# Latent attention: the causal corner masked by eight extra rows of the score product, query and key pages in fixed tiles

## The chip, the cores and the metric

The kernel runs on one core of a Trainium2 chip. The metric is the device time of one execution in microseconds (us). The core's engines run side by side, each with its own queue of instructions: PE multiplies matrices (its weight loads are listed as PEld), DVE does vector work, ACT evaluates functions, POOL does further vector work, and SP issues most of the DMA transfers. PE writes its products to PSUM; everything else lies in SBUF, which has 128 partitions.

## The reference

One encoder layer on a sequence of 1024 rows of 1024 values. The mixer has eight latent heads and eight chunk-band heads; a gated MLP with a short convolution follows. Only the latent heads' attention is touched:

```python
def mla_attention(q, k, v):                      # q, k: 8 heads of 96 values (64 + 32 rotary)
    scale = Dq ** -0.5
    key_chunk = jnp.arange(S) // CHUNK           # CHUNK = 64
    def block(args):                             # one block of 128 queries
        qi, i = args
        s = jnp.einsum('bqhd,bkhd->bhqk', qi, k) * scale
        q_chunk = (i * Q_BLOCK + jnp.arange(Q_BLOCK)) // CHUNK
        mask = key_chunk[None, :] <= q_chunk[:, None]
        s = jnp.where(mask[None, None], s, NEG_INF)
        p = jax.nn.softmax(s, axis=-1)
        return jnp.einsum('bhqk,bkhd->bqhd', p, v)
```

A query block of 128 rows holds two chunks of 64. Keys up to the end of the block are used, and the first 64 queries must not see the last 64 of these keys: a corner of 64 x 64 in each block's score tile.

## The kernel before

**Stages.** The program first computes the modulation and the projections, then the chunk-band heads, then the latent heads, then the output projection and the MLP. In the profile the latent score products (L807) start between 367 us and 583 us; their values products (L895) follow until about 599 us.

**Numbers.** A 32-bit operand is split into a high and a low half, and a product is made of three: high x high, high x low, low x high. All three accumulate in one PSUM tile.

**Pages.** A page is 512 rows of queries or of keys, transposed, so that the head's values lie on the partitions. `qk_page` (L736) builds one for the latent heads: four transposes on PE into PSUM (`page_psum`, L733), the high half by ACT (L741 for queries, L745 for keys), the low half by DVE (L742, L746). A latent page uses 96 partitions. `ca_pages` (L749) does the same for a pair of chunk-band heads and uses all 128. Query pages come from a tag with four buffers (`q2`), key pages from a tag with three buffers, each buffer with high and low half; the buffers are taken in turn.

**Units and tiles.** A `Unit` is one head and one group `g` of four query blocks. There are 16 chunk-band units, then 16 latent ones in the order group 0, group 1 of each head. Each has four score tiles, so that there are 64 latent score tiles. For a latent tile `scores` (L778) issues the products (L807), sets the masked corner of the PSUM tile to 1e30 (DVE, L825), takes the row minimum (DVE, L826; scores are negated, so that the minimum plays the part of the maximum), the exponential and its row sum (ACT, L833), the reciprocal and its scaling (DVE, L835 and L836), then the high half of the probabilities (POOL, in the helper at L73) and the low half (DVE, L855), and their transpose by DMA (L867). `values`, three tiles later, multiplies the transposed probabilities with the values (PE, L895), and ACT and DVE (L904, L905) bring the sum out. The score tiles alternate between two PSUM buffers.

**Order.** The units' tiles are written out in a loop; between them `pace` adds steps of the low-priority projections (`fillers`: among them `f_up` with L666 to L694, `f_oca` with L154 to L156). Pages of the next unit are prepared at the third tile of a unit if the projection that they need has been written out by then, otherwise right before the unit's first tile; the first latent head's two pages of each kind are in the latter case. The order of instructions on each engine is then set by a planner that goes by priorities (`tc.high_priority`), by dependencies and by a model of each instruction's time, so that other work of an engine may stand between two instructions that follow each other in the text.

Of the kernel before, what the change touches and what calls it, by code (L numbers as in the profile page):

```python
# [14 lines left out]
F32R = mybir.dt.float32r  # L15
# [7 lines left out]
MUL, ADD, SUB, MIN, MAX = ALU.mult, ALU.add, ALU.subtract, ALU.min, ALU.max  # L23

P = 128
D = 1024
S = 1024
NT = S // P
# [2 lines left out]
NF = FF // P  # L31
EPS = 1e-6
BIG = 1e30
QR, KVR, ROPE, NOPE, VD = 256, 128, 32, 64, 64
QK = NOPE + ROPE
HD = 64
# [28 lines left out]
def layer_kernel(ctx, tc, I, out):  # L65
    nc = tc.nc
    pe, act, dve, pool, sp = nc.tensor, nc.scalar, nc.vector, nc.gpsimd, nc.sync

    def f32(ap):
        return ap.bitcast(F32)  # L70
# [27 lines left out]
    ident = cst.tile([P, P], F32, name="ident")  # L98
# [11 lines left out]
    gk_m = cst.tile([P, 1], F32, name="gk_m")  # L110
# [36 lines left out]
    def pgtile(shape, dt, name):  # L147
        return apg.tile(shape, dt, name=name, tag="pg", bufs=6)
# [133 lines left out]
    for d in range(ND):  # L282
# [22 lines left out]
        for t in range(NT):  # L305
            h, j = divmod(t, 4)
# [7 lines left out]
    at = att.__enter__()  # L314
# [313 lines left out]
    mq, mk, mv = {}, {}, {}  # L628
# [94 lines left out]
                sp.dma_start(part_d[t][:, n * 512:(n + 1) * 512], o[:])  # L723


    def q2(name):
        return at.tile([P, 512], F32R, name=name, tag="Q2", bufs=4)

    def page_psum(src, name, rows, tag="T"):
        pt = ps.tile([P, 512], F32, name=f"{name}_ps", tag=tag, bufs=TB)  # L730
        with tc.issue_after(first[0]):
            for j in range(4):
                pe.transpose(pt[:rows, j * P:(j + 1) * P], src(j), ident[:])  # L733
        return pt

    def qk_page(src, name, rows, tag, bufs, gain):  # L736

        pt = page_psum(src, name, rows)
        if gain is None:
            hi, lo = q2(f"{name}h"), q2(f"{name}l")  # L740
            act.activation(hi[:rows], pt[:rows], AF.Copy)  # L741
            dve.tensor_tensor(lo[:rows], pt[:rows], f32(hi[:rows]), op=SUB)  # L742
            return hi, lo
        pg = at.tile([P, 2, 512], F32R, name=name, tag=tag, bufs=bufs)
        act.activation(pg[:rows, 0], pt[:rows], AF.Copy, scale=gain)  # L745
        dve.scalar_tensor_tensor(pg[:rows, 1], pt[:rows], gain, f32(pg[:rows, 0]), op0=MUL, op1=SUB)  # L746
        return pg

    def ca_pages(p, g):  # L749

        qn = qns[p, g]
        half = (slice(0, 64), slice(64, 128))
        pt = page_psum(lambda j: qn[:, j, 0:128], f"q{p}_{g}", P)
        if p == g == 0:
            pk_ = page_psum(lambda j: qn[:, j, 128:256], f"k{p}_{g}", P, "pv")
        qh = [q2(f"qh{p}_{g}_{o}") for o in range(2)]
        ql = qlow[0], qlow[1 + g]
        for o in range(2):
            act.activation(qh[o][half[o]], pt[half[o]], AF.Copy)
            dve.tensor_tensor(ql[o][half[o]], pt[half[o]], f32(qh[o][half[o]]), op=SUB)  # L760
            pool.tensor_copy(qh[o][half[1 - o]], f32(qh[o][half[o]]))
        pt = pk_ if p == g == 0 else page_psum(lambda j: qn[:, j, 128:256], f"k{p}_{g}", P)
        kk = at.tile([P, 2, 512], F32R, name=f"k{p}_{g}", tag="K", bufs=3)
        for o in range(2):
            act.activation(kk[half[o], o], pt[half[o]], AF.Copy, scale=gk_ca[half[o]])
            dve.scalar_tensor_tensor(kk[half[1 - o], o], pt[half[o]], gk_ca[half[o]], f32(kk[half[o], o]),
                                     op0=MUL, op1=SUB)
        return (qh, ql), kk

    class Unit:  # L770
# [7 lines left out]
        def scores(u, i):  # L778

            qpg, kpgs = u.pages()  # L780
            bias = u.bias() if u.band else None
            lo = max(0, i - 4) if u.band else 0
            n = (i - lo + 1) * P
# [3 lines left out]
            with tc.high_priority(offset=OFF_S):  # L787
                s = ps.tile([P, 1024], F32, name=f"s{nm}", tag="S", bufs=2)
                n0 = max(0, min(4, i + 1) - lo) * P
                n1 = n - n0  # L790
                c0 = 512 - n0 if n1 else 0
                segs = [(c0, lo * P, n0, 0)] if n0 else []
                if n1:
                    segs.append((512, max(lo, 4) * P - 512, n1, 1))
                q = slice((i % 4) * P, (i % 4 + 1) * P)
                rs_ = slice(u.base, u.base + u.rows)
                if u.band:
                    qh, ql = qpg
                    for x, a in enumerate((qh[u.odd], ql[u.odd])):
                        for c, ko, w, kh in segs:  # L800
                            last = pe.matmul(s[:, c:c + w], a[:, q], kpgs[kh][:, u.odd, ko:ko + w],
                                             start=(x == 0), stop=(x == 1))
                else:
                    for a in range(2):
                        for c, ko, w, kh in segs:
                            for b in range(2 - a):
                                last = pe.matmul(s[:, c:c + w], qpg[a][rs_, q], kpgs[kh][rs_, b, ko:ko + w],  # L807
                                                 start=(a == 0 and b == 0), stop=(a == 1))
                trail.append(last.ins)
                sv = s[:, c0:c0 + n]  # L810
                m = cst.tile([P, 1], F32, name=f"m{nm}", tag="m", bufs=4)
                if u.band:
                    if i >= 4:
                        dve.memset(sv[64:128, 0:64], BIG)
                    w = min(n, 256)
                    if n > 256:
                        m0 = cst.tile([P, 1], F32, name=f"m0{nm}", tag="m0", bufs=4)
                        dve.tensor_reduce(m0[:], sv[:, :n - 256], axis=AX.X, op=MIN)
                        init = m0[:]
                    else:  # L820
                        init = 3e38
                    anchor["dve"] = dve.tensor_tensor_reduce(sv[:, n - w:n], sv[:, n - w:n], bias[:, 256 - w:256], 1.0, init,  # L822
                                             ADD, MIN, accum_out=m[:]).ins
                else:
                    dve.memset(sv[0:64, n - 64:n], BIG)  # L825
                    anchor["dve"] = dve.tensor_reduce(m[:], sv, axis=AX.X, op=MIN).ins  # L826
                short = n <= (640 if u.band else 512)
                pieces = [(0, n)] if short else [(0, 512), (512, n)]
                if n <= 640:
                    pr = at.tile([P, 640], F32, name=f"P{nm}", tag="P", bufs=P_BUFS)  # L830
                else:
                    pr = pgtile([P, 1024], F32, f"P{nm}")
                act.activation(pr[:, :n], sv, AF.Exp, bias=m[:], scale=-1.0, accum_out=rsum[:, 0:1])  # L833
            with tc.high_priority(offset=OFF_P):
                dve.reciprocal(ri[:], rsum[:, 0:1])  # L835
                dve.tensor_scalar(ri[:], ri[:], PSCALE, None, op0=MUL)  # L836
                for x, (p0, p1) in enumerate(pieces):
                    w = p1 - p0
# [89 lines left out]
    def mask_bias(hd):  # L928
        b = biases[hd]
        dve.tensor_scalar(b[:], b[:], pk[:, C_RB + hd:C_RB + hd + 1], -1.0, op0=SUB, op1=MUL)  # L930
        dve.memset(b[0:64, 192:256], BIG)

# [23 lines left out]
    def mla_unit(gr, hh, g):  # L956
        o = hh % 2

        def prep():
            q = qk_page(lambda j: mq[gr, (4 * g + j) // 2][:, j % 2, hh, :], f"mq{gr}{hh}_{g}", QK, "Q", 2, None)  # L960
            k = qk_page(lambda j: mk[gr, (4 * g + j) // 2][:, j % 2, hh, :], f"mk{gr}{hh}_{g}", QK, "K", 3, gk_m[:QK])
            pages[gr, hh, g] = (q, k)
        u = Unit(f"m{gr}{hh}", 0, QK,
                 lambda: (pages[gr, hh, g][0], [pages[gr, hh, i][1] for i in range(g + 1)]),
                 lambda j: mv[gr, j // 2][:, j % 2, hh].rearrange("p a b -> p (a b)"),
                 g, False, None, o, oT_d[2 * gr + hh // 2], ("m", gr))
        u.prep = prep
        u.need = [f"up{gr}"] if g == 0 else ["up1"]
        u.needv = []
        return u  # L970
# [60 lines left out]
    for n in range(len(tiles) + DEPTH):  # L1031
        if n < len(tiles):
            u, i = tiles[n]
# [3 lines left out]
            if i % 4 == 2 and n + 2 < len(tiles):  # L1037
                v = tiles[n + 2][0]
# [4 lines left out]
        if n >= DEPTH:  # L1043
            u, i = tiles[n - DEPTH]
# [178 lines left out]
    for k in range(4):  # L1223
# [4 lines left out]
        for q, wl, wh in rows0:  # L1228
            product(q[:, 512:], wl, "b12", add=k > 0, ks=[k], skip=True)
            last = product(q[:, 512:], wh, "b22", add=True, ks=[k])  # L1230
# [347 lines left out]
    for t in range(4):  # L1578
        o = dl.tile([P, 512], F32, name=f"oe{t}", tag="oe", bufs=3)
# [80 lines left out]
```

## Time and profile before

| | |
|---|---|
| median of three runs | 1318.42 us (1316.21 to 1319.64) |
| the profiled execution | 1320.49 us |
| its span, first to last instruction | 1318.7 us |
| mean granted PE clock | 0.964 of full speed |
| latent score products, first and last start | 367.7 and 583.1 us |
| latent row minima (L826) | 64, 267 to 1226 ns |
| latent corner memsets (L825) | 64, 112 ns each |

The profile gives, for each engine, the time in which it was busy, groups of instructions by line and shape with their mean duration, what each engine waited for, and the instructions in order of time. A wait is put down to the instruction whose end came last. "Issue" stands for time in which the engine waited for nothing that the profile shows.

### The profile page before, as it was taken

The numbers are of one execution on the slowest core, as the hardware profiler recorded it, in microseconds if no ns is written. First come the engines' busy times: TensorE is split into PE (matmuls) and PEld (weight loads), VectorE is DVE, ScalarE is ACT, GpSimd is POOL, SyncE is SP. The second block draws the span as 40 slices with busy tenths as digits, with TensorE's granted clock in tenths as the row PEclk, the third lists the DMA queues.
The fourth block names the chain that finished last, engine by engine and source line by source line (L and its number), as shares of the span: only waits on it lengthen the run. The fifth ranks groups of instructions, "written<-read, shape, count | busy, mean of one in ns | idle before, by whom it ended". The sixth has DMA issues, their size and how long they took to land. (4 is left out here: it accounts for less than half of the span.)

```text
span 1318.7 us, 18701 instructions
## 1 busy us (share of the span) xinstructions
PE 1192.2 (90%) x6168; PEld 993.5 (75%) x6168; DVE 1080.2 (82%) x1864; ACT 627.3 (48%) x1148; POOL 597.4 (45%) x629
## 2 busy tenths in 40 slices
PE   4899889988768987868899999999999999999998
PEld 3789889878546766756777888888888886888886
DVE  6979988887589988874789888888889887687667
ACT  5455654455656454542375444443444444433331
POOL 5485773586687643454616444554444431000000
PEclk9999898989879899989999999999999999999999
DMA  8416768665233687789602334333343337943441
GB/s 326 144 55 153 170 146 187 157 161 119 48 85 62 148 165 155 146 173 300 265 17 84 125 104 136 112 114 125 93 131 106 128 104 245 394 145 109 128 160 64
DMA packets 223690, 190.83 MB, mean 145 GB/s; under 512 B 148709, under 2 KB 166373, under 8 KB 223593
## 3 DMA queue, kind: packets, MB, share of 16 engines
q1 hardware_dynamic: 223592, 189.64, 50.5%
q8 instruction: 48, 0.79, 0.2%
q14 instruction: 50, 0.40, 0.1%
HBM read 117.50 MB, written 37.49 MB: 118 GB/s over the span
## 5 line engine op out<-in xcount | busy, mean ns | idle before, releaser
L77 ACT ACTIVATE dnP<-dnr 128x1024 fp32r<-128x1024 f32 x73 | 77.5, 1064 | 116.1 <-PE dnA_P L1471 46.4
L1443 DVE TENSOR_TENSOR dnP<-dnr,dnP 128x1024 fp32r<-128x1024 f32 x72 | 88.7, 1236 | 51.8 <-ACT dnP L77 51.7
L73 POOL TENSOR_SCALAR hlm<-Pm,rim 128x512 f16<-128x512 f32 (+3 forms) x96 | 67.9, 716 | 66.7 <-issue 22.5
L84 POOL TENSOR_TENSOR wf<-wu,wf 128x512 fp32r<-128x512 f32 x22 | 38.6, 1752 | 116.6 <-ACT wf L77 116.6
L84 POOL TENSOR_TENSOR wb<-wu,wb 128x512 fp32r<-128x512 f32 x22 | 44.9, 2040 | 84.5 <-ACT wb L77 56.9
L1305 DVE SCALAR_TENSOR_TENSOR u<-c,cvp,u 128x1023 f32<-128x1023 f32 x44 | 55.8, 1310 | 27.6 <-ACT u L1304 24.8
L855 DVE SCALAR_TENSOR_TENSOR hlm<-Pm,rim,hlm 128x512 f16<-128x512 f32 (+3 forms) x96 | 68.7, 728 | 6.4 <-POOL hlm L73 6.2
L73 POOL TENSOR_SCALAR hlc<-Pc,ric 128x640 f16<-128x640 f32 (+2 forms) x64 | 49.7, 780 | 47.3 <-DVE ric L836 18.4
L833 ACT ACTIVATE Pc<-sc,mc 128x640 f32<-128x640 f32 (+2 forms) x64 | 42.3, 661 | 54.3 <-DVE mc L822 37.2
L833 ACT ACTIVATE Pm<-sm,mm 128x128 f32<-128x128 f32 (+3 forms) x64 | 47.2, 737 | 37.3 <-DVE mm L826 20.0
L895 PE MATMUL pvm<-PTm,vt 128*128 128x256 f16 (+1 forms) x320 | 43.6, 284 | 22.6 <-DMA PTm<-hlm 21.6
L1304 ACT ACTIVATE u<-c,cvp 128x1024 f32<-128x1024 f32 x44 | 52.4, 1238 | 23.6 <-DVE c L1403 16.7
L895 PEld LDWEIGHTS <-vt 128*128 128x128 f16 x320 | 31.3, 105 | 35.9 <-DMA PTm<-hlm 15.8
L855 DVE SCALAR_TENSOR_TENSOR hlc<-Pc,ric,hlc 128x640 f16<-128x640 f32 (+2 forms) x64 | 51.3, 806 | 8.4 <-POOL hlc L73 8.2
L77 ACT ACTIVATE wc<-ws 128x512 fp32r<-128x512 f32 x21 | 13.3, 632 | 93.1 <-DVE ws L1153 87.2
L154 PE MATMUL ipq<-wq_s,hT 128*128 128x256 f32 x192 | 56.4, 294 | 0.0
L1306 DVE SCALAR_TENSOR_TENSOR u<-c,cvp,u 128x1022 f32<-128x1022 f32 x44 | 55.5, 1301 | 0.0
L155 PE MATMUL ipq<-wq_s,hT 128*128 128x256 f32 x192 | 55.0, 287 | 0.0
L156 PE MATMUL ipq<-wq_s,hT 128*128 128x256 f32 x192 | 55.0, 287 | 0.0
L1470 PE MATMUL dnA_P<-dnP 128*128 128x512 f32 x132 | 51.3, 389 | 0.0
L1471 PE MATMUL dnA_P<-dnP 128*128 128x512 f32 x132 | 51.3, 389 | 0.0
L1469 PE MATMUL dnA_P<-dnP 128*128 128x512 f32 x132 | 51.2, 389 | 0.0
(441 smaller groups left out, 4420.5 us busy)
## 6 DMA issues: line engine op xcount, KB each, us to landing
wu<-w_up SPq DMA_DIRECT2D x44, 512.0 KB, 3.6
dnr<-g_d SPq DMA_DIRECT2D x73, 256.0 KB, 2.7
aw<-w_ada SPq DMA_DIRECT2D x48, 256.0 KB, 3.2
g_d<-u SPq DMA_DIRECT2D x22, 512.0 KB, 3.0
dnr<-w_down SPq DMA_DIRECT2D x44, 256.0 KB, 5.4
adaw<-w_ada_a SPq DMA_DIRECT2D x16, 512.0 KB, 6.2
x<-x SPq DMA_DIRECT2D x16, 512.0 KB, 9.4
g_d<-gs SPq DMA_DIRECT2D x22, 256.0 KB, 2.8
```

Of the source, the lines that this page charges most:

```text
L73: pool.tensor_scalar(o, i, s, 1.0, op0=MUL, op1=MUL)
L77: act.activation(o, i, AF.Copy)
L84: (pool if eng == "p" else dve).tensor_tensor(o, i, f32(hi), op=SUB)
L154: pe.matmul(pt, sh, mh, start=(start and i == 0), stop=False)
L155: pe.matmul(pt, sh, ml, start=False, stop=False)
L156: last = pe.matmul(pt, sl, mh, start=False, stop=(stop and i == n - 1))
L833: act.activation(pr[:, :n], sv, AF.Exp, bias=m[:], scale=-1.0, accum_out=rsum[:, 0:1])
L855: dve.scalar_tensor_tensor(hl[:, w:2 * w], pp, ri[:], hl[:, :w], op0=MUL, op1=SUB)
L895: last = pe.matmul(dst, u.vst(j), mov, start=(x == 0), stop=(x == len(todo) - 1), skip_group_check=True)
L1305: dve.scalar_tensor_tensor(u[:, 1:], c[:, :S - 1], cvp[:, cv + 1:cv + 2], u[:, 1:], op0=MUL, op1=ADD)
L1306: dve.scalar_tensor_tensor(u[:, 2:], c[:, :S - 2], cvp[:, cv:cv + 1], u[:, 2:], op0=MUL, op1=ADD)
L1443: r = f(*a, **k)
```

## The change

The corner's memset is taken out. In its place each latent page gets eight further partitions, 96 to 103, one for each of the eight query blocks. In the high half of a query page, row r holds 1 in the first 64 columns of block r and 0 elsewhere; in the high half of a key page, row r holds 2^100 in the last 64 columns of block r and 0 elsewhere. The product of the two high halves runs over 104 rows and so adds 2^100 to the corner of each block and 0 to all other scores; the other two products stay at 96 rows.

So that these rows are written only once, pages no longer rotate. There are two query tiles (high and low) for each group, and three key tiles: 0 and 1 for group 0 of even and odd heads, 2 for group 1. The chunk-band heads use the same tiles, and as these fill all 128 partitions, the rows are written when a tile is first used by a latent head: two POOL instructions (a memset and a scaled copy from the identity) for each of two query and three key tiles.

```diff
+MASK = 2.0 ** 100
...
-    def q2(name):
-        return at.tile([P, 512], F32R, name=name, tag="Q2", bufs=4)
+    qfix = [[at.tile([P, 512], F32R, name=f"qp{g}{o}") for o in range(2)] for g in range(2)]
+    kfix = [at.tile([P, 2, 512], F32R, name=f"kp{n}") for n in range(3)]
+    MROW = slice(QK, QK + NT)
+
+    def mask_rows(page, g, second, value):
+        v = page[MROW].rearrange("p (t h c) -> p t h c", t=4, h=2)
+        pool.memset(f32(v[:, :, 1 - second]), 0.0)
+        pool.tensor_scalar(v[:, :, second], ident[MROW, QK + 4 * g:QK + 4 * g + 4].unsqueeze(2).to_broadcast([NT, 4, 64]),
+                           value, 0.0, op0=MUL, op1=ADD)
...
-    def qk_page(src, name, rows, tag, bufs, gain):
+    masked = set()
+
+    def qk_page(src, name, rows, g, slot, gain):
 
         pt = page_psum(src, name, rows)
+        pg = qfix[g][0] if gain is None else kfix[slot][:, 0]
+        if (gain is None, slot) not in masked:
+            masked.add((gain is None, slot))
+            mask_rows(pg, g, int(gain is not None), 1.0 if gain is None else MASK)
         if gain is None:
-            hi, lo = q2(f"{name}h"), q2(f"{name}l")
+            hi, lo = qfix[g]
...
-        pg = at.tile([P, 2, 512], F32R, name=name, tag=tag, bufs=bufs)
+        pg = kfix[slot]
...
-        qh = [q2(f"qh{p}_{g}_{o}") for o in range(2)]
+        qh = qfix[g]
...
-        kk = at.tile([P, 2, 512], F32R, name=f"k{p}_{g}", tag="K", bufs=3)
+        kk = kfix[(2 * p + g) % 3]
...
-                rs_ = slice(u.base, u.base + u.rows)
...
-                                last = pe.matmul(s[:, c:c + w], qpg[a][rs_, q], kpgs[kh][rs_, b, ko:ko + w],
+                                rr = slice(0, QK if a or b else QK + NT)
+                                last = pe.matmul(s[:, c:c + w], qpg[a][rr, q], kpgs[kh][rr, b, ko:ko + w],
                                                  start=(a == 0 and b == 0), stop=(a == 1))
...
-                    dve.memset(sv[0:64, n - 64:n], BIG)
                     anchor["dve"] = dve.tensor_reduce(m[:], sv, axis=AX.X, op=MIN).ins
...
-            q = qk_page(lambda j: mq[gr, (4 * g + j) // 2][:, j % 2, hh, :], f"mq{gr}{hh}_{g}", QK, "Q", 2, None)
-            k = qk_page(lambda j: mk[gr, (4 * g + j) // 2][:, j % 2, hh, :], f"mk{gr}{hh}_{g}", QK, "K", 3, gk_m[:QK])
+            q = qk_page(lambda j: mq[gr, (4 * g + j) // 2][:, j % 2, hh, :], f"mq{gr}{hh}_{g}", QK, g, g, None)
+            k = qk_page(lambda j: mk[gr, (4 * g + j) // 2][:, j % 2, hh, :], f"mk{gr}{hh}_{g}", QK, g, 2 if g else hh % 2, gk_m[:QK])
```

## The prediction

> **What bounds the kernel now.** First the page's busy times and its slices, to see which engine is full and where.
>
> ```profile
> PE 1192.2 (90%) x6168; PEld 993.5 (75%) x6168; DVE 1080.2 (82%) x1864; ACT 627.3 (48%) x1148; POOL 597.4 (45%) x629
> PE   4899889988768987868899999999999999999998
> DVE  6979988887589988874789888888889887687667
> ```
>
> Each slice is 33 us. From slice 20 on, counted from 0 (about 660 us), PE is full: that is the channel mixer, which the change does not touch. In slices 11 to 17 neither PE nor DVE is. The latent heads lie there, and the change acts only there. So I asked for busy time by stretch (columns: stretch, its length, then PE, PEld, DVE, ACT, POOL busy with counts, granted clock, DMA share, GB/s), first the whole stage, then three parts of it.
>
> ```profile
> 365.00:590.00 225.00, 184.35 (x984) 144.55 (x985) 191.38 (x481) 124.53 (x278) 131.08 (x152) 0.91 0.63 134
> 365.00:390.00 25.00, 16.69 (x59) 12.29 (x59) 19.16 (x49) 16.16 (x43) 22.59 (x24) 0.73 0.31 90
> 410.00:420.00 10.00, 7.71 (x37) 5.85 (x36) 9.97 (x30) 5.31 (x16) 9.38 (x8) 0.83 0.59 111
> 520.00:530.00 10.00, 7.45 (x47) 6.12 (x46) 6.47 (x22) 4.94 (x13) 4.61 (x7) 1.00 0.87 167
> ```
>
> DVE works 191.38 of 225 us, 85%, a little more than PE. The limit moves: POOL at first (22.59 of 25), then DVE (9.97 of 10), later nobody. Who waits for whom in this stage (us in total, times, longest) shows rings instead of one full engine:
>
> ```profile
> ACT Pm L833 <- DVE mm L826: 20.0, 18, 3.5
> PE pvm L895 <- DMA PTm<-hlm: 17.1, 14, 3.6
> PE sm L807 <- ACT Pm L833: 10.5, 9, 2.1
> DVE sm L825 <- PE sm L807: 10.2, 12, 3.6
> ```
>
> One ring is scores, row minimum (L826), exponential (L833), and then the score bank is free for the tile after next; the other is split probabilities, DMA transpose, values product. Row minimum and split both need DVE. An instruction taken off DVE therefore counts with about DVE's share, not in full and not with zero.
>
> **Part 1: 64 memsets leave DVE.** The group, and two ways in which a memset sits in DVE's queue (columns: start, duration):
>
> ```profile
> L825 DVE MEMSET sm<- 64x64 f32 x64 | 7.2, 112 | 10.8 <-PE sm L807 10.2
> 369.33 0.11 DVE L825 MEMSET sm<- 64x64 f32 x1
> 369.36 0.35 DVE L685 TENSOR_REDUCE uss<-kraw 128x4 f32<-128x260 f32 x1
> 370.70 0.60 DVE L826 TENSOR_REDUCE mm<-sm 128x1 f32<-128x128 f32 x2
> ...
> 442.51 0.11 DVE L825 MEMSET sm<- 64x64 f32 x1
> 442.65 0.76 DVE L905 SCALAR_TENSOR_TENSOR om<-pvm,vabm,om 64x512 f32<-64x512 f32 x1
> ...
> 581.88 0.11 DVE L825 MEMSET sm<- 64x64 f32 x1
> 582.03 1.09 DVE L826 TENSOR_REDUCE mm<-sm 128x1 f32<-128x896 f32 x1
> ...
> 584.61 0.11 DVE L825 MEMSET sm<- 64x64 f32 x1
> 584.64 0.66 DVE L84 TENSOR_TENSOR wo<-wor,wo 128x512 fp32r<-128x512 f32 x1
> ...
> 585.69 1.20 DVE L826 TENSOR_REDUCE mm<-sm 128x1 f32<-128x1024 f32 x1
> ```
>
> Start to start, 38 of the 64 hold DVE for about 0.03 us only: the next instruction, unrelated, begins inside the memset (first at 369.33, last at 584.61). 21 hold it 0.14 to 0.15 us (first at 442.51, last at 581.88), mostly because their own row minimum comes next. Behind the other 5 the next instruction waits for something else; I give them 0.15. Sum: 38 x 0.032 + 21 x 0.146 + 5 x 0.15 = 1.2 + 3.1 + 0.75 = 5.0 us of DVE. With DVE's share of the stage, 191.38 / 225 = 0.85, that is 4.3 us of time. Ends: 0 (the rings never wait for DVE) and 9.6 us (64 x 0.15, every memset with the long gap). I take 4.3 because the gaps are seen one by one. What is late next is the same row minimum, waiting for the same product: the 10.2 us that the memset waits for PE pass to L826 unchanged.
>
> The Trainium skill, "VectorE: DVE Perf Modes", section "The DRAIN you can't avoid", says that the next operation does not start until the pipe of the last one is empty, and advises to minimize the count of operations rather than their waits. By that every memset would be worth the long gap, 9.6 us in all; the successor at 369.36, inside the memset, speaks against it, the one at 582.03 for it.
>
> The memset also parts the product from the row minimum. Over the 64 pairs the mean is 0.85 us (first 369.33 to 370.70, last 584.61 to 585.69), with other DVE work in between. Without the memset the order written for DVE can put the row minimum there at once; but the instructions that it overtakes are then later by as much. I count 0 and keep both ends: a gain up to PE's whole wait for the exponential, 10.5 us, and a loss worked out under the rivals.
>
> **Part 2: eight more rows in the product, on PE.** No product is added; 96 rows become 104 in the one of three that takes both high halves.
>
> ```profile
> L807 PE MATMUL sm<-mk,mq_1h 96*128 96x512 f32 x80 | 27.1, 439 | 7.5 <-ACT Pm L833 7.5
> L154 PE MATMUL oc<-wo,ch 128*128 128x512 f32 x64 | 26.9, 421 | 0.3 <-ACT ch L77 0.3
> ```
>
> In the same stage a product of 128 rows takes 421 ns and one of 96 rows 439 ns; 104 lies between: 0. The rows do not change the count of weight loads either.
>
> **Part 3: ten POOL instructions, once.** Each of the five pages in use gets a memset and a scaled copy of 8 partitions x 256 at its first latent use. POOL has no row with 8 partitions; the nearest by elements of a partition:
>
> ```profile
> L101 POOL MEMSET ones<- 128x128 f32 x1 | 0.2, 205 | 0.0
> L915 POOL MEMSET qlow<- 64x512 f32 x3 | 1.5, 518 | 0.1
> L522 POOL TENSOR_SCALAR lat<-lat,mr 128x256 f32<-128x256 f32 x8 | 3.8, 480 | 0.4
> ```
>
> A memset of 256 lies a third of the way from 205 to 518 ns, 0.31 us; with 0.48 for the copy a pair is 0.79 us, five pairs 4.0 us. Two pairs come before the first head's first pages (query page at 361.8), two before its second pages (382.4), one later. They wait for the last chunk-band product that reads the page, long over (324.7), so POOL's queue is not held up.
>
> ```profile
> L741 ACT ACTIVATE mq_0h<-mq_ps x8: 579/594/598, 361.8 to 547.8; 96x512 fp32r<-96x512 f32 x8
> L741 ACT ACTIVATE mq_1h<-mq_ps x8: 580/591/596, 382.4 to 559.1; 96x512 fp32r<-96x512 f32 x8
> L801 PE MATMUL sc<-k,qlow x96: 220/320/735, 86.2 to 324.7; 128*128 128x128 f32 x24, 128*128 128x256 f32 x24, 128*128 128x384 f32 x24, 128*128 128x512 f32 x24
> 361.54 0.20 POOL L119 TENSOR_SCALAR uss<-uss 128x8 f32<-128x8 f32 x1 [1.37 <-DVE uss L685]
> 369.80 0.20 POOL L119 TENSOR_SCALAR uss<-uss 128x8 f32<-128x8 f32 x1 [1.81 <-DVE uss L685]
> ```
>
> The added wait is PE's, for the first product on a page; behind it stand the head's other products and the low-priority projections, and the row minimum on DVE waits with them. POOL has gaps (1.37 us before 361.54, 1.81 before 369.80) that hide some pairs, but it is 90% busy from 365 to 390. I count one pair, +0.8 us. Ends: 0, and the four early pairs in full, 3.2 us.
>
> **Part 4: fixed pages.** Same number and size of pages (four query, three key), so the same memory. Between two uses of a page lie the same tiles as with three or four buffers in turn: the second group's key page is written at the second tile after its last reader, and so was the buffer that came next in turn. 0.
>
> **Sum.** -4.3 + 0 + 0.8 + 0 = -3.5 us. The profiled execution took 1320.49 us (span 1318.7), 2.1 above the median of the runs; the difference is carried over to the median 1318.42: 1314.9 us. 0.3% of this kernel, about what a measurement can tell from no change, is 4.0 us, so the forecast sits at that edge.
>
> **The rivals.** (a) *The score ring tightens.* Row minima move up by the gap of part 1, 0.85 us, at each of the 9 places where PE waits for an exponential; 10.5 us of wait shrink by 7.6. For it: exponentials wait 20.0 us for row minima. Against: DVE is full in stretches like 410 to 420, where an earlier row minimum only makes another instruction late. Time: 1314.9 - 7.6 = 1307.3.
> (b) *Every operation costs its drain.* The skill's rule above as a mechanism: 9.6 instead of 4.3 us, so 1318.42 - 9.6 + 0.8 = 1309.6. Against it 38 gaps of 0.03 us.
> (c) *Slower: the row minimum overtakes the split.* With no memset ahead of it, L826 enters DVE's queue before a split (L855) that stood in between, and holds it for its duration:
>
> ```profile
> L826 DVE TENSOR_REDUCE mm<-sm x64: 267/745/1226, 370.7 to 585.7; 128x1 f32<-128x128 f32 x8, 128x1 f32<-128x256 f32 x8, 128x1 f32<-128x384 f32 x8, 128x1 f32<-128x512 f32 x8
> ```
>
> The split feeds the transposes, for which PE waits already at 14 places. If at each the split comes 0.745 us later, PE's wait grows by 10.4 us: 1314.9 + 10.4 = 1325.3. It decides once the wait of the values product for its transposes goes above 17.1 + 7.5 = 24.6 us. For it: transposes are the larger wait of PE. Against: the order can leave the split where it is.
> (d) *Nothing comes off.* In stretches like 520 to 530 DVE is idle a third of the time and the DMA engines are busy 0.87; if the transposes set the pace throughout, the DVE time saved becomes idle time: 1318.4 to 1319.2.
>
> **How the numbers follow.** Forecast 0.43, (a) 0.17, (b) 0.05, (c) 0.22, (d) 0.13. The forecast's own spread (-7 to 0) lies half beyond 4.0 us: 0.215 to faster, 0.215 to same. Faster: 0.215 + 0.17 + 0.05 = 0.435; same: 0.215 + 0.13 = 0.345; slower: 0.22. Forecast alone: 1311 to 1318.5. The range goes to the middle of (a) and of (c), 1307 to 1325.5, leaving out half of each, 0.2.
>
> **What would show it.** DVE 1864 to 1800 instructions, POOL 629 to 639, the L807 group in two forms, 96 and 104 rows, of equal duration. Right: DVE's busy time in the latent stage down by 5 to 7 us, the stage shorter by about 3.5, the rest of the kernel as long as before. (a) shows in PE's wait for the exponential under 5 us, (c) in its wait for transposes over 24.6. Wrong: a first latent score more than 1 us later than before while POOL is full, products of 104 rows that take longer, or a stage before 360 us or after 605 us that changes its length, for which I have no term.

## The result, and the profile after

The changed kernel took 1314.41 us (median of 10 runs, 1311.25 to 1316.71), the kernel before 1319.11 us on the same chip (1316.21 to 1325.26). The ratio is 0.9959, 95% interval 0.9943 to 0.9975: faster by 5.4 us, 3.3 to 7.5 (the two medians are 4.7 us apart). The forecast was 1314.9, 3.5 us less than its own starting point of 1318.42. The profiled execution took 1314.38 us (span 1312.6; before 1320.49 and 1318.7), at a mean granted clock of 0.963 (before 0.964).

First the lines of the changed kernel's page that answer to those shown before: busy times, then the slices of PE and DVE.

```profile
PE 1195.0 (91%) x6168; PEld 992.1 (76%) x6168; DVE 1071.0 (82%) x1800; ACT 624.9 (48%) x1148; POOL 600.2 (46%) x639
PE   4899999989768889968989999999999999999998
DVE  6979989878589678875899889888888987687667
```

DVE has 64 instructions fewer (1800) and POOL ten more (639). In the latent stage PE is a little fuller in slices 15 and 16 (9 and 9, before 7 and 8); from slice 21 on its digits are the same. The same stretches of the latent stage as before (columns: stretch, length, then PE, PEld, DVE, ACT, POOL busy with counts, granted clock, DMA share, GB/s):

```profile
365.00:590.00 225.00, 184.57 (x989) 141.65 (x990) 183.54 (x418) 122.87 (x277) 134.04 (x154) 0.92 0.64 135
365.00:390.00 25.00, 15.56 (x59) 10.55 (x60) 18.87 (x50) 16.14 (x43) 22.30 (x25) 0.80 0.32 90
410.00:420.00 10.00, 8.31 (x49) 6.48 (x50) 9.73 (x24) 6.84 (x20) 9.66 (x11) 1.00 0.44 84
520.00:530.00 10.00, 9.65 (x64) 7.79 (x64) 9.31 (x26) 5.66 (x13) 5.58 (x8) 1.00 0.83 149
```

DVE's busy time in the stage fell by 191.38 - 183.54 = 7.8 us; the 64 memsets were 7.2 us of it. The last stretch shows that more than the memsets changed: from 520 to 530 us DVE was busy 6.47 us before and 9.31 us now. Other work runs there, and the stretch is the same on the clock, not in the program. The waits of the stage (us in total, times, longest):

```profile
ACT Pm L846 <- DVE mm L839: 23.4, 17, 4.9
PE sm L821 <- ACT Pm L846: 11.8, 11, 2.9
PE pvm L908 <- DMA PTm<-hlm: 10.9, 10, 3.0
DVE mm L839 <- PE sm L821: 8.8, 5, 4.6
```

PE's wait for the DMA transposes fell from 17.1 to 10.9 us, and the waits of the score ring rose: exponential for row minimum from 20.0 to 23.4, product for exponential from 10.5 to 11.8. The row minima, the mask rows of the key pages on POOL, and the score products, together and by shape:

```profile
L839 DVE TENSOR_REDUCE mm<-sm x64: 264/745/1225, 369.5 to 578.9; 128x1 f32<-128x128 f32 x8, 128x1 f32<-128x256 f32 x8, 128x1 f32<-128x384 f32 x8, 128x1 f32<-128x512 f32 x8
L733 POOL MEMSET kp<- x3: 307/307/308, 246.7 to 309.3; 8x256 f32 x3
L734 POOL TENSOR_SCALAR kp<-ident x3: 406/411/513, 247.1 to 309.6; 8x256 fp32r<-8x256 f32 x3
L821 PE MATMUL sm<-kp,qp x288: 218/392/774, 367.3 to 577.3; 96*128 96x512 f32 x38, 104*128 104x512 f32 x38, 104*128 104x128 f32 x16, 96*128 96x128 f32 x16
L821 PE MATMUL sm<-kp,qp 96*128 96x512 f32 x96 | 35.8, 421 | 0.0
L821 PE MATMUL sm<-kp,qp 104*128 104x512 f32 x48 | 22.2, 465 | 5.9 <-ACT Pm L846 5.7
```

The stage, from the first row minimum to the last, takes 578.9 - 369.5 = 209.4 us against 585.7 - 370.7 = 215.0 before: 5.6 us shorter. Its first row minimum is 1.2 us earlier, but not because anything before it got faster: it stands where the first memset stood (369.3 us before, 369.5 now). Counted from the first score product, 367.7 us before and 367.3 now, to the last row minimum, the stage takes 211.6 us against 218.0, 6.4 us less. So nearly all of the 6.1 us between the two spans lies in the stage: 0.4 came before it, and what follows it is 0.7 us longer in this pair of executions. The mask rows of the key pages were written between 246.7 and 310 us, before the latent stage.

### The profile page after: what moved, and what is told of

Read it like the earlier page. It is cut to its first block, busy times and chain, and to the rows that moved or that the text cites. A ratio compares the mean times of both kernels' runs of the same rounds, so it can differ in the third digit from the quotient of the medians.

```text
span 1312.6 us, 18651 instructions
## 1 busy us (share of the span) xinstructions
PE 1195.0 (91%) x6168; PEld 992.1 (76%) x6168; DVE 1071.0 (82%) x1800; ACT 624.9 (48%) x1148; POOL 600.2 (46%) x639
## 5 line engine op out<-in xcount | busy, mean ns | idle before, releaser
L821 PE MATMUL sm<-kp,qp 96*128 96x512 f32 (+7 forms) x288 | 71.2, 375 | 13.2 <-ACT Pm L846 11.8
L74 POOL TENSOR_SCALAR hlc<-Pc,ric 128x640 f16<-128x640 f32 (+2 forms) x64 | 49.4, 775 | 44.1 <-DVE ric L849 12.9
L821 PEld LDWEIGHTS sm<-kp,qp 96*128 96x128 f32 (+1 forms) x288 | 49.1, 198 | 25.0 <-ACT Pm L846 16.7
L846 ACT ACTIVATE Pm<-sm,mm 128x128 f32<-128x128 f32 (+3 forms) x64 | 47.3, 739 | 38.8 <-DVE mm L839 23.4
L1317 ACT ACTIVATE u<-c,cvp 128x1024 f32<-128x1024 f32 x44 | 52.3, 1238 | 23.4 <-DVE c L1416 16.5
L908 PE MATMUL pvm<-PTm,vt 128*128 128x256 f16 (+1 forms) x320 | 42.9, 281 | 14.7 <-DMA PTm<-hlm 10.9
L839 DVE TENSOR_REDUCE mm<-sm 128x1 f32<-128x128 f32 (+3 forms) x64 | 47.3, 746 | 9.3 <-PE sm L821 8.8
L908 PEld LDWEIGHTS <-vt 128*128 128x128 f16 x320 | 30.6, 103 | 28.8 <-issue 11.8
```

The costliest lines, as they stand in the source:

```text
L74: pool.tensor_scalar(o, i, s, 1.0, op0=MUL, op1=MUL)
L821: last = pe.matmul(s[:, c:c + w], qpg[a][rr, q], kpgs[kh][rr, b, ko:ko + w], start=(a == 0 and b == 0), stop=(a == 1))
L908: last = pe.matmul(dst, u.vst(j), mov, start=(x == 0), stop=(x == len(todo) - 1), skip_group_check=True)
```

## Experiments

### Which part does it

The theory was that the memset alone is worth what was measured, and the rows and the fixed pages nothing. Its rivals: the pages or the rows carry part of it, or the memsets are worth more than DVE's share of their slots. Three kernels divide the change.

The fixed pages alone (against the changed kernel):

```diff
-        if (gain is None, slot) not in masked:
-            masked.add((gain is None, slot))
-            mask_rows(pg, g, int(gain is not None), 1.0 if gain is None else MASK)
...
-                                rr = slice(0, QK if a or b else QK + NT)
+                                rr = slice(0, QK)
...
+                    dve.memset(sv[0:64, n - 64:n], BIG)
```

> The kernel before, with the pages in fixed tiles; the corner's memset stays and no mask rows are written, so the output is that of before. Theory 1 (the memsets' slots on DVE are the gain): same as before, within 2 us. Theory 2 (the gain is that the row minimum follows the product directly): same as before, within 2 us. Theory 3 (the gain is a new order of the whole stage, which the fixed pages may bring as well): it may come out several us from before, towards the changed kernel at -5.

Measured: ratio 1.0008 [0.9991, 1.0025].

The kernel before with nothing but the memset left out:

```diff
-                    dve.memset(sv[0:64, n - 64:n], BIG)
```

> The kernel before without the corner's memset and without anything in its place: the corner of each latent block is not masked. Pages rotate as before. Theories 1 and 2: as fast as the changed kernel or 1 us faster (no POOL work for mask rows), -5 to -6 us against before. Theory 3: anywhere between -8 and +3, not near the changed kernel.

Measured: 0.9962 [0.9943, 0.9981].

The changed kernel with the memset put back:

```diff
+                    dve.memset(sv[0:64, n - 64:n], BIG)
```

> The changed kernel with the corner's memset put back ahead of the row minimum. Theories 1 and 2: the gain is gone, 0 to +1 us against before. Theory 3: not bound to before; if the fixed pages or rows are the gain it stays at -5.

Measured: 1.0005 [0.9983, 1.0027].

So fixed pages, mask rows and the ten POOL instructions cost nothing that can be measured, and taking the memset out gives the whole difference (0.9962 beside 0.9959). The 104-row products are no longer either. They are the first product of each tile for a block of keys, and a first product has the longer mean at 96 rows as well (in e1 462 ns, the other two 415 and 412). The products of 512 columns in e3, by shape, and in e1, where all have 96 rows:

```profile
L821 PE MATMUL sm<-kp,qp 96*128 96x512 f32 x96 | 35.5, 415 | 0.0
L821 PE MATMUL sm<-kp,qp 104*128 104x512 f32 x48 | 21.7, 456 | 7.8 <-ACT Pm L847 7.8
```

```profile
L818 PE MATMUL sm<-kp,qp 96*128 96x512 f32 x144 | 48.5, 430 | 7.8 <-ACT Pm L844 7.8
```

Count times mean: 96 x 0.415 + 48 x 0.456 = 61.7 us with the rows, 144 x 0.430 = 61.9 us without.

### The slot on DVE

If the price is DVE's slot, a memset that nothing in the latent heads depends on should cost the same.

```diff
+    junk64 = cst.tile([P, 64], F32, name="junk64")
...
+                    dve.memset(junk64[0:64, :], BIG)
```

> The changed kernel with a DVE memset of 64 x 64 at the old place, but into an unrelated tile in SBUF: DVE is charged for 64 memsets, the row minimum does not depend on them. Theory 1: most of the gain is gone, -1 to 0 us against before (0.03 us of slot each would leave up to -3). Theory 2: the gain stays, -4 to -5 us. Theory 3: anywhere.

Measured: 1.0051 [1.0031, 1.0070]. It is no test of that. The group of these memsets:

```profile
L840 DVE MEMSET junk<- x64: 112/112/112, 0.8 to 32.0; 64x64 f32 x64
  PE p_ada L294: 12.9, 1
```

The planner, which found no dependency on the latent heads, put all 64 at the start of the program, and the modulation's products waited 12.9 us for them. The run is a miss, but it showed that an edit can move work to quite another place.

Doubling the memset in the kernel before:

```diff
                     dve.memset(sv[0:64, n - 64:n], BIG)
+                    dve.memset(sv[0:64, n - 64:n], BIG)
```

> The kernel before with two equal memsets of the corner in a row for each tile. The planner writes another order than before from the start of the latent heads on. Theory 1 (the memsets' slots on DVE): as much again as the removal gave, +4 to +6 us against before. Theory 2 (what counts is the distance from product to row minimum): it grows by about 0.15 us for each tile, +2 to +5 us. Theory 3 (the order written by the planner decides, and any change of the text draws a new one): anywhere between -5 and +8, not bound to the number of memsets.

Measured: 1.0036 [1.0021, 1.0051], 4.7 us slower, close to the forecast's 4.3 with the other sign. The next two runs shook that agreement. The mask rows written by DVE instead of POOL:

```diff
-        pool.memset(f32(v[:, :, 1 - second]), 0.0)
-        pool.tensor_scalar(v[:, :, second], ...
+        dve.memset(f32(v[:, :, 1 - second]), 0.0)
+        dve.tensor_scalar(v[:, :, second], ...
```

> The changed kernel with the ten instructions for the mask rows on DVE instead of POOL. Theories 1 and 2: within 2 us of the changed kernel, -3 to -6 us against before (ten more DVE instructions of under 0.4 us, once). Theory 3: it has an order of its own from about 255 us on and may come out several us away from the changed kernel, to either side.

Measured: 1.0027 [1.0015, 1.0039]: slower than the kernel before, though the 64 memsets are gone and only ten short instructions have come, all before 316 us. And the memset kept in the changed kernel for half of the heads, first 0 to 3, then 4 to 7:

```diff
+                    if u.vs[1] == 0:        # e8: == 1
+                        dve.memset(sv[0:64, n - 64:n], BIG)
```

> The changed kernel with the corner's memset kept in the first four latent heads (32 of 64 tiles), beside the mask rows. Theories 1 and 2: half the gain, -2 to -4 us against before, and this one and its counterpart (memset kept in the last four heads) add up to the changed kernel's gain. Theory 3: the two need not add up.

> The changed kernel with the corner's memset kept in the last four latent heads. Theories 1 and 2: half the gain, -2 to -4 us against before. Theory 3: not bound to that; it follows the changed kernel's order until about 470 us, so it is near the changed kernel up to there, and what follows is open.

Measured: 0.9942 [0.9922, 0.9962] with the memsets of the first half kept, 1.0008 [0.9993, 1.0022] with those of the second. Against the kernel before, leaving out the second half's memsets gives 5.8 per mille, the first half's -0.8. The sum, 5.0, agrees with the 4.1 of all of them within the intervals, but about half for each was forecast. The kept halves hold nearly the same slots (18 short and 10 long gaps in e7's trace, 19 and 11 in e8's), so the price of a memset alone cannot part them like this. The row minima of e6 and of e7:

```profile
L839 DVE TENSOR_REDUCE mm<-sm x64: 268/749/1212, 374.5 to 581.1; 128x1 f32<-128x128 f32 x8, 128x1 f32<-128x256 f32 x8, 128x1 f32<-128x384 f32 x8, 128x1 f32<-128x512 f32 x8
```

```profile
L841 DVE TENSOR_REDUCE mm<-sm x64: 267/748/1225, 373.6 to 579.5; 128x1 f32<-128x128 f32 x8, 128x1 f32<-128x256 f32 x8, 128x1 f32<-128x384 f32 x8, 128x1 f32<-128x512 f32 x8
```

In both the stage starts 4 to 5 us later than in the changed kernel and is shorter, 206.6 and 205.9 us against 209.4. Yet e6 is slow and e7 fast: in e6 the output projection's last product starts at 651.8 us, in the changed kernel at 644.9 and in e7 at 645.3. What makes e6 slow therefore does not lie between the row minima, where the memsets were.

### The order by itself

Comparing the sequences of DVE and ACT instructions in the traces (memsets set aside) showed the reason. They are identical in the kernel before, e1 and e3: call that order M. They are identical in the changed kernel and e2: order N. M and N part behind DVE's 794th instruction, at 369 us, where the latent heads begin. The other edits got orders of their own: e4 from the start, e6 behind the 570th instruction (254 us), e5 from the latent heads on. The order of e7 is M, and that of e8 is N, up to DVE's 1034th instruction (about 497 us), and only then their own. So a measured difference holds two things: the memsets, and the order that the planner draws once they are gone.

To part them, four kernels were given a fixed order on all five engines: each instruction gets an edge, without a semaphore, to its predecessor in a recorded order. Where memsets are added, each is set right before its row minimum.

```diff
+    for eng, code in ORDER.items():            # recorded order of each engine
...
+        for n in order:
+            i = text[int(n)]
+            if i.name in corner:               # a row minimum that has its memset
+                chain.append(corner[i.name])
+            chain.append(i)
+        for a, b in zip(chain, chain[1:]):
+            tc.add_manual_dep(b, a.name, ...NoSync...)
```

Order M without memsets, order N with all 64, and the order of e7 (order H) without and with all 64:

> The changed kernel (mask rows, no memset) with the instructions of every engine pinned to the order in which the kernel with rows and memset has them, which is the order of before on DVE and ACT. Theory 1 (the memsets' slots on DVE): the slots are gone, -4 us against before. Theory 3 (the order decides): it stays at before, 0 +- 1.5 us. In both the row minimum keeps its late place, about 1.9 us behind its product.

> The changed kernel with all 64 memsets put back, each right before its row minimum, and the instructions of every engine pinned to the order of the changed kernel. Theory 1: 64 slots of 0.15 us, 9.3 us of DVE, by its share of 0.85 some +8 us against the changed kernel, +2 to +4 against before. Theory 3: it keeps the changed kernel's gain, -5 +- 1.5 us against before.

> The changed kernel (no memset) pinned to the order of the kernel that kept the memset in the first four heads, the fastest so far at -7.6 us. Theory 1: 32 more slots are gone, -9.5 to -10 us against before. Theory 3: it stays at -7.6 +- 1.5 us.

> The same order with all 64 memsets, each right before its row minimum. Theory 1: against the kernel without memsets in this order 9.3 us of DVE more, +8 us, so about -2 us against before. Theory 3: -7.6 +- 1.5 us against before.

| order | without memsets | with 64 memsets | price of the memsets |
|---|---|---|---|
| M (the kernel before) | f1: 0.9974 [0.9958, 0.9990] | 1 (before); e3: 1.0005 [0.9983, 1.0027] | 3.4 us (1.3 to 5.5) |
| N (the changed kernel) | after: 0.9959 [0.9943, 0.9975] | f2: 1.0014 [0.9998, 1.0030] | 7.2 us, about 3 either way |
| H (e7) | f3: 0.9910 [0.9893, 0.9927] | f4: 0.9938 [0.9923, 0.9953] | 3.7 us, about 3 either way |

The prices are differences of ratios times 1319 us; where two measured ratios are subtracted, the bound adds their half intervals as squares. Of what was expected, theory 1, the slots, came nearest in f1, f2 and f3: -3.4, +1.8 and -11.9 us against before. f4, at -8.2 us, is a miss for it (about -2) and lies in the band of theory 3, the order. e7 itself, with order H and 32 memsets, gives one more price beside f3: 0.9942 to 0.9910, 4.2 us, about 3.5 either way.

The traces show that the pinning did what it should: on PE, DVE, ACT, POOL and the DMA queue, f1 has the sequence of the kernel before, f2 that of the changed kernel, f3 and f4 that of e7 (memsets and mask rows set aside). No kernel was pinned with nothing else changed, so a cost of the pinning itself is not excluded in M and N, where one side of the pair is not pinned; in H both are.

The table reads both ways. Down its first column only the order changes: without memsets M and N are 0.0015 apart, 2.0 us, less than the bound; H is 8.4 us faster than M. Across a row only the memsets change.

The slots: measured from the start of a memset to the start of the next DVE instruction, order M has, in the profile of before, the 38 short and 21 long gaps of the prediction, 4.3 us together, and 5 behind which DVE waits. In f2 and f4 each memset has its own row minimum next, and all 64 gaps are long, 0.146 us, 9.35 us together. From f2's timeline (start, duration):

```profile
466.67 0.11 DVE L840 MEMSET sm<- 64x64 f32 x1 [4.65 <-PE sm L822]
466.82 0.82 DVE L841 TENSOR_REDUCE mm<-sm 128x1 f32<-128x640 f32 x1
467.65 0.11 DVE L840 MEMSET sm<- 64x64 f32 x1
467.79 0.96 DVE L841 TENSOR_REDUCE mm<-sm 128x1 f32<-128x768 f32 x1
```

So f2 and f4 test more slot time than the kernel before had: 7.2 / 9.35 = 0.77 of it reached the end in order N, 3.7 / 9.35 = 0.40 in order H, and 3.4 / 5.0 = 0.68 in order M. The bounds for M and N hold 0.85, those for H (0.08 to 0.72) don't.

The traces give the same picture by the length of the stage, from the first score product to the last row minimum. Order M with memsets: 218.0, 219.0 and 218.1 us (before, e1, e3), without 213.5 (f1). Order N without: 211.6 and 211.6 (after, e2), with 219.1 (f2). Order H without: 209.4 (f3), with 211.6 (f4). These are single executions, but kernels of the same order and the same memsets agree within 1.0 us. By this measure the memsets cost 4.5 to 5.5 us in M, 7.5 in N and 2.2 in H, and without them N is 1.9 us shorter than M. When the stage starts says less: up to there before, e1, e3, e7, f1, f3 and f4 have the same order, and their first score products start anywhere from 364.7 (f3) to 370.0 us (e7).

The busy times of the stretch from 365 to 590 us, in f1, f2, f3 and f4 (the columns of the stretches above):

```profile
365.00:590.00 225.00, 180.54 (x991) 141.68 (x991) 189.67 (x423) 125.18 (x279) 135.13 (x154) 0.93 0.65 137
```

```profile
365.00:590.00 225.00, 181.55 (x980) 139.11 (x979) 191.52 (x480) 122.14 (x275) 129.38 (x152) 0.94 0.61 129
```

```profile
365.00:590.00 225.00, 183.81 (x996) 144.27 (x995) 187.90 (x418) 122.98 (x274) 130.07 (x151) 0.91 0.68 142
```

```profile
365.00:590.00 225.00, 182.82 (x991) 142.65 (x991) 200.67 (x485) 123.49 (x276) 130.68 (x155) 0.92 0.64 135
```

f4 keeps DVE busy for 200.67 us, 89% of the stretch, more than any other, and is still faster than the kernel before at 191.38. A fuller DVE alone thus does not make a kernel of this family slower. That it matters what DVE does while PE needs it is a reading that no run isolates. f3 is the fastest of all: 1306.83 us (5 runs, 1306.10 to 1309.96), faster than the kernel before by 11.9 us and than the changed one by about 6.5. Its product work is the same as the changed kernel's; only the order differs. M and H are one order up to DVE's 1034th instruction, and what H gains lies behind it: from there to the last row minimum f1 takes 87.8 us and f3 83.0, from the first score product to there 125.7 and 126.4.

## Why the prediction was right

**The memsets' slots, -4.3 us.** At a fixed order (M, f1) the price was 3.4 us, 1.3 to 5.5. The count of gaps by kind gave the right size in this order; the share of 0.85 is not borne out as a rule, since in order H the bounds of what came out exclude it. e2 and e3 show that rows and pages have no part in it. That the time came out at 1314.41 beside 1314.9 is partly luck. The change was 5.4 us, where 3.5 was forecast, and the median of the kernel before was 0.7 us higher than the three runs from which the forecast started. Of the 5.4 us, 3.4 are the memsets at the old order, where 4.3 was forecast, and 2.0 are the new order, which had no term and whose bound of 3 us holds zero too; the 0.8 us of POOL, forecast the other way, did not come.

The marks that were set: the stage was to be 3.5 us shorter, and from its first score product it is 6.4, of which 4.5 came at the old order (f1) and 1.9 with the new one. DVE's busy time in the stretch fell by 7.8 us (5 to 7 forecast), but this mark is a poor one: in f1 it fell by 1.7 us only, with 58 instructions fewer for 64 memsets left out, as later work had moved into the stretch. The first latent score did not start later (367.3 and 367.7 us).

**The row minimum next to its product, 0.** The row minimum did move up, and the rest of its ring gave most of that back. Means over the 64 tiles, from the starts and ends of products, row minima and exponentials in the traces:

| us | before | f1 (M) | after (N) | e6 | e4 | f3 (H) |
|---|---|---|---|---|---|---|
| a tile's products, first start to last end | 1.16 | 1.13 | 1.40 | 1.37 | 1.49 | 1.12 |
| last product's end to row minimum | 1.94 | 1.77 | 1.10 | 1.07 | 0.99 | 1.50 |
| row minimum's end to exponential | 0.68 | 0.73 | 0.93 | 0.79 | 0.92 | 0.78 |
| exponential's end to the next product in its bank | 1.61 | 1.63 | 1.77 | 1.92 | 2.04 | 1.74 |
| the ring with the two operations | 6.87 | 6.74 | 6.69 | 6.62 | 6.92 | 6.63 |

The last row adds 0.75 us for the row minimum and 0.74 for the exponential, the same in all. In the changed kernel the row minimum did take the memset's old place, 0.84 us nearer to its product. The other legs of the ring grew by 0.24 + 0.25 + 0.16 = 0.65 us. That they grew because what the row minimum overtakes comes later is the prediction's argument; no run isolates it. The ring runs 32 times in each of the two banks: 32 x (6.87 - 6.69) = 5.8 us. That is the shorter stage divided by legs, and no second measurement of it. Most of the 0.18 us is there in f1 too, with the old order: its row minimum stands 0.67 us farther from the product than in the changed kernel, and its ring is only 0.05 us longer. So the 0 of that step was right as a net, to within the 2 us of the order.

**POOL, +0.8 us.** Wrong in place, harmless in size. The step set the pairs between 361 and 390 us, at the first latent use of a page. The planner put the rows between 246.7 and 310 us, as soon as the page's last reader allowed, and nobody waited for them; e2, without any of them, took the same time as the changed kernel. The prices of the two instructions, 0.307 and 0.411 us, are near the 0.31 and 0.48 of the rows used.

**Products of 104 rows, 0; fixed pages, 0.** Shown by e3 and e1 (1.0005 and 1.0008, both intervals around 1).

**The rivals.** (a) did not come: PE's wait for exponentials went up, 10.5 to 11.8 us, where it was to fall under 5. (b) was to be worth 9.6 us; order M gave 3.4, so it is refuted for the gaps of the kernel before. In f2, where each memset is forced ahead of its own row minimum, the long gap is paid 64 times and 7.2 of 9.35 us reach the end: that rival's price needs that neighbour. The Trainium skill, "VectorE: DVE Perf Modes", section "Two Vector instructions with no wait between them", states, as a model, that a held instruction starts only when every earlier Vector instruction has finished; the section that the prediction cites adds that a next operation that is not held starts earlier (the advice on the count of operations stands in that page's section "Rules for kernel authors"). The 38 successors in the kernel before that start 0.03 us after a memset of 0.112 us agree. (c) did not come: the wait for transposes fell to 10.9 us, where 24.6 was the mark. (d), nothing, is excluded by 0.9943 to 0.9975, and at the old order by f1's 0.9958 to 0.9990.

**What had no term** is the redrawn order. Here it happened to be worth 2 us or less; in e7's order the same instructions are 8.4 us faster than in the old one, and e6, also without the 64 memsets, is 7.0 us slower than f1 (1.0027 to 0.9974; e6 has its mask rows on DVE). The range of 1307 to 1325.5 covered that by way of the two ring rivals, not by this reason. By which of its swaps the order of e7 is better was not tried.

## What to carry to other kernels

Price a small instruction by the gap from its start to the next start on its engine, kind by kind, times the engine's share of the stage: 0.68 and 0.77 of the slots came out in two orders, 0.40 in a third, where the share said 0.85, so take the result as a size and not as a figure. Where a planner sets the order, an edit can draw a new one: of the nine kernels that were not pinned (the changed one and e1 to e8) only e1 and e3 kept the old order. Here orders differ by up to 0.8% on the same instructions (f2 and f4), more than the edit is worth: compare the edit at a pinned order before believing its price, and treat the order as a choice to search, since the best order found (f3) gained more than the change did.

## What was not expected of the hardware

- A memset of 8 partitions x 256 on POOL takes 307 ns, near the 309 ns that the memsets of 128 partitions x 128 (205 ns) and 64 x 512 (518 ns) give by interpolation: the small count of partitions made no difference that shows. On DVE the same memset takes 272 ns in e6.
- The long gap behind a DVE memset of 112 ns, 0.146 us, came at every one of the 64 places in f2 and f4, where the row minimum of its own tile follows. Where the planner placed the memsets, 39 of the 64 gaps in e3 were about 0.03 us, with other work behind.
